# Seven-product tiles: two block sums by accumulating transfers, and 15 of 22 tiles instead of 12

## The chip, the cores and the metric
The kernel runs on one core of a Trainium2 chip. The metric is the device time of one execution in microseconds; lower is better. The engines are TensorE (PE), VectorE (DVE), ScalarE (ACT), GpSimd (POOL) and SyncE (SP), which issues most transfers; each works through its own instructions in order and waits for others by semaphores.

## What is computed
The reference is a two-layer model on 512 tokens of width 1024: in each layer a feed-forward part, a mixer (attention), and another feed-forward part, then a norm. The change touches the feed-forward parts alone:

```python
def _swiglu(x, w_gate, w_up, w_down):
    return (jax.nn.silu(x @ w_gate) * (x @ w_up)) @ w_down
...
    for l in range(DEPTH):
        x = x + 0.5 * _swiglu(_rms_norm(x, ffn1_norm[l]), ffn1_w_gate[l], ffn1_w_up[l], ffn1_w_down[l])
        h = _rms_norm(x, mix_norm[l])
        ...
        x = x + 0.5 * _swiglu(_rms_norm(x, ffn2_norm[l]), ffn2_w_gate[l], ffn2_w_up[l], ffn2_w_down[l])
```

All is float32. The inner width D_FF is 2816, which is 22 tiles of 128.

## The kernel before
The program runs the stages f0, e, f1, f2, m, f3: four feed-forward stages and two mixers. Activations lie transposed, features in the 128 partitions and 512 tokens in the columns. Each float32 factor is kept as a high part (rounded by a copy on ACT) and a low part (the rest, by a subtraction on DVE), and a product is three matmuls: high by high, low by high, high by low (`mm3`).

A feed-forward stage goes over 22 tiles f of the inner width, in two halves of 11. After each half the down projection of that half runs (264 matmuls). An ordinary tile loads its two weight tiles (gate and up, 512 KB each, names w, wh, wl), and makes 2 x 8 x 3 = 48 matmuls of 512 columns. For the tiles in the list `SEVEN`, gate and up together are taken as a matrix of 2 by 2 blocks A11, A12 (gate, first and second half of the width) and A21, A22 (up, R21 and R22 in the code), times the activations as 2 by 2 blocks, and are made by seven block products instead of eight, 7 x 4 x 3 = 84 matmuls of 256 columns. The products need A11, A12, A22 and four sums of weight blocks: S1 = R21 + R22, S2 = S1 + A11, S3 = A11 + R21, S4 = A12 + S2. Each of the seven then gets its high and its low part. The combined activations T12 and T34 are made once per stage (`combine`).

`chunk` hands out the weights in the order of use and fetches two entries of the list ahead of the one in use; a seven-product tile is one entry, an ordinary one two. The raw weights (w), their high parts (wh) and low parts (wl) have three buffers of 1024 columns each; a seven-product tile takes three pairs of wh and wl (A11 with S2, S1 with S3, A12 with S4) and a pair of its own for A22 (w3h, w3l, one buffer). The matmuls accumulate in PSUM banks pa, pb (two each), pt (three) and pc (one). A scheduler lays out each engine's instructions when the program is built, so the order on an engine is fixed, and an instruction that waits holds up all behind it on its engine.

Names that the steps below use: L160 and L161 split an ordinary weight tile (copy on ACT, low part on DVE); in `fetch_seven`, L170 and L171 load gate and up, L174 adds blocks on DVE, L180 and L181 split. In `seven`, L328 to L342 read the products out of PSUM (fm, fv, fn, fg) and L360, L376, L377 finish the tile. L251 is the power on GpSimd that makes a norm's factor, L231 its sums of squares. In the changed file lines from the end of `fetch_seven` on stand 13 lines further down, and the splits of a seven-product tile are L193 and L194.

Of the kernel before, what the change touches and what calls it, by code (L numbers as in the profile page):

```python
# [3 lines left out]
P = 128  # L4
D, SEQ, FF = 1024, 512, 2816
# [3 lines left out]
F32, F32R = mybir.dt.float32, mybir.dt.float32r  # L9
AF, OP, AX = mybir.ActivationFunctionType, mybir.AluOpType, mybir.AxisListType  # L10
# [14 lines left out]
def raw(ap):  # L25
    return ap.bitcast(F32)
# [2 lines left out]

SEVEN = (4, 5, 7, 8, 10, 11, 13, 14, 16, 17, 19, 20)

FFNS = {"f0": ("f1", 0, 0), "f1": ("f2", 0, 2), "f2": ("f1", 1, 3), "f3": ("f2", 1, 5)}

# [20 lines left out]
def flat(plan):  # L56
    return [u for _, fills in plan for f in fills for u in f.split()]


def keys(u):  # L60

    mla, c, n = u.isupper(), u[0].lower(), u[1:]
    if c == "v" and n in "aA":
        return [("ev_vsw", i) for i in range(3)]
    n = int(n)
    if mla:
        return {"L": [("mla_in", n)], "W": [("mla_uq", n)], "Y": [("mla_ukv", n)],
                "O": [("mla_out", n)]}.get(u[0], [])
    return {"q": [("ev_in", n)], "k": [("ev_in", n)], "s": [("ev_in", 4 + n)], "o": [("ev_out", n)],
            "c": [("cmp_w1", n, 0), ("cmp_w1", n, 1)], "v": [("ev_vb", n, 0), ("ev_vb", n, 1)]}.get(c, [])  # L70
# [7 lines left out]
class Core:  # L78
# [47 lines left out]
    def plan(self, stages):  # L126

        todo = []
        for st in stages:
            if st in FFNS:  # L130
                name, l, _ = FFNS[st]
                for h in range(2):
                    for f in range(h * HF, h * HF + HF):
                        if f in SEVEN:
                            todo.append(("seven", name, l, f))
                        else:
                            todo += [(name + "_g", l, f), (name + "_u", l, f)]
                    todo += [(name + "_d", l, h, c) for c in range(HF)]
            else:
                for u in flat(EVEN if st == "e" else MLA):  # L140
                    todo += keys(u)
        self.todo, self.ready, self.ahead = todo, [], 2

    def fetch(self):

# [15 lines left out]
        nc.vector.tensor_tensor(l[:, :cols], w[:, :cols], raw(h[:, :cols]), OP.subtract)  # L161
        self.ready.append((key, (h, l)))

    def fetch_seven(self, name, l, f):

        nc, kp, sb = self.nc, self.keep, self.sb
        g, u = [kp.tile([P, 1024], F32, name="w", bufs=3) for _ in range(2)]
        nc.sync.dma_start(g, self.a[name + "_g"][l, f])  # L170
        nc.sync.dma_start(u, self.a[name + "_u"][l, f])  # L171
        a11, a12, r21, r22 = g[:, :SEQ], g[:, SEQ:], u[:, :SEQ], u[:, SEQ:]
        s1, s2, s3, s4 = [sb.tile([P, SEQ], F32, name=f"s{i}") for i in range(1, 5)]
        add = lambda o, a, b: nc.vector.tensor_tensor(o, a, b, OP.add)  # L174
        out = {}

        def parts(blocks, h, l):
            for i, (n, src) in enumerate(blocks):
                c = slice(i * SEQ, i * SEQ + SEQ)
                nc.scalar.activation(h[:, c], src, AF.Copy)  # L180
                nc.vector.tensor_tensor(l[:, c], src, raw(h[:, c]), OP.subtract)  # L181
                out[n] = h[:, c], l[:, c]

        def pair():
            return [kp.tile([P, 1024], F32R, name=n, bufs=3) for n in ("wh", "wl")]
        add(s1, r21, r22)
        add(s2, s1, a11)
        parts((("A11", a11), ("S2", s2)), *pair())
        add(s3, a11, r21)
        parts((("S1", s1), ("S3", s3)), *pair())  # L190
        add(s4, a12, s2)
        parts((("A12", a12), ("S4", s4)), *pair())
        parts((("A22", r22),), *[sb.tile([P, SEQ], F32R, name=n) for n in ("w3h", "w3l")])  # L193
        return out  # L194

    def chunk(self, *key):
# [148 lines left out]
    def ffn(self, name, l, gi, then=None):  # L345

        nc = self.nc
        with self.tc.tile_pool(name="ff", bufs=1, reuse_waits="tile") as sb:
# [3 lines left out]
            for half in range(2):  # L352
                ah, al = [], []
                for i in range(HF):
                    f = half * HF + i
                    a = sb.tile([P, SEQ], F32, name="fa", bufs=2)
                    if f in SEVEN:
                        g, n = self.seven(sb, ("seven", name, l, f), xs, T, R)
# [607 lines left out]
def layout(np, i):  # L966

    i = {k: np.asarray(v) for k, v in i.items()}
    d = {"x": i["x"][0].T}
    d["g"] = np.concatenate(  # L970
        [v.reshape(-1, P).T for v in (i["ffn1_norm"][0], i["mix_norm"][0], i["ffn2_norm"][0], i["ffn1_norm"][1],
                                      i["mix_norm"][1], i["ffn2_norm"][1], i["final_norm"],
                                      i["mla_q_norm"][0], i["mla_kv_norm"][0])]
        + [np.zeros((P, 1), np.float32)], axis=1)
    for n in ("1", "2"):
        for s, t in (("gate", "g"), ("up", "u")):
            w = i[f"ffn{n}_w_{s}"]
            d[f"f{n}_{t}"] = w.reshape(2, KT, P, NF, P).transpose(0, 3, 2, 1, 4).reshape(2, NF, P, 1024)
        w = i[f"ffn{n}_w_down"].reshape(2, 2, HF, P, KT, P).transpose(0, 1, 4, 2, 3, 5)
        d[f"f{n}_d"] = w.reshape(2, 2, HF, 8, P, P).transpose(0, 1, 2, 4, 3, 5).reshape(2, 2, HF, P, 1024)  # L980

    def feat(w):

        k, n = w.shape[0] // P, w.shape[1] // P
        return w.reshape(k, P, n, P).transpose(2, 1, 0, 3).reshape(n, P, k * P)

    def out_parts(w, parts):

        w = w.reshape(8, P, KT, P)
        res = []  # L990
        for pairs in parts:
            n = len(pairs)
            v = w[list(pairs)].transpose(2, 0, 1, 3).reshape(n, 8, P, P)
            res.append(v.transpose(0, 2, 1, 3).reshape(n, P, 1024))
        return np.concatenate(res)

    def tok(w, n):

        w = w.reshape(KT, P, -1)
        pad = -KT % n  # L1000
        if pad:
            w = np.concatenate([w, np.zeros((pad,) + w.shape[1:], w.dtype)])
        return w.reshape(-1, n, P, w.shape[2]).transpose(0, 2, 1, 3).reshape(len(w) // n, P, -1)
    w = i["ev_w_in"][0]
    cols = [w[:, c:c + n] for c, n in ((C_QA, 512), (C_KC, 128), (C_VC, 128), (C_KS, 128), (C_KW, 128),
                                       (C_QB, 512), (C_KB, 512))]
    d["ev_in"] = feat(np.concatenate(cols, axis=1))
    d["ev_vsw"] = tok(np.concatenate([w[:, C_VS:C_VS + 128], w[:, C_VW:C_VW + 128], w[:, C_G:C_G + 24]], axis=1), 3)
    d["ev_vb"] = np.stack([tok(w[:, C_VB + 256 * j:C_VB + 256 * j + 256], 4) for j in range(2)])
    d["ev_out"] = out_parts(i["ev_w_out"][0], EV_PARTS)  # L1010
    w = np.stack([i[f"nsa_cmp_pos_{s}"][0].reshape(16, 2, 64).transpose(2, 1, 0) for s in "kv"], axis=1)
    d["pos"] = np.concatenate([w, w])
    d["cmp_w1"] = np.stack([i[f"nsa_cmp_{s}_w1"][0].reshape(2, 8, P, P).transpose(0, 2, 1, 3).reshape(2, P, 1024)
                            for s in "kv"])
    d["cmp_w2"] = np.stack([np.concatenate([i[f"nsa_cmp_{s}_w2"][0]] * 2, axis=1) for s in "kv"], axis=1)
    w = i["mla_w_in"][0]
    d["mla_in"] = feat(np.concatenate([w[:, :384]] + [w[:, 384:416]] * 4, axis=1))
    w = i["mla_w_uq"][0].reshape(2, P, 16, 96)
    n, r, z = w[..., :64], w[..., 64:], np.concatenate([w[..., 80:], w[..., 64:80]], axis=-1)
    w = np.stack([np.concatenate([n, r, z], axis=-1)[:, :, 0::2], np.concatenate([r, z, n], axis=-1)[:, :, 1::2]],  # L1020
                 axis=3)
    d["mla_uq"] = w.reshape(2, P, 4, 4, P).transpose(2, 1, 3, 0, 4).reshape(4, P, 1024)
    w = i["mla_w_ukv"][0].reshape(P, 2, 8, 2, 64).transpose(1, 0, 3, 2, 4)
    d["mla_ukv"] = w.reshape(2, P, 1024)
    d["mla_out"] = out_parts(i["mla_w_out"][0], ML_PARTS)
    d.update(constants(np))
    return {k: np.ascontiguousarray(v) for k, v in d.items()}
# [18 lines left out]
```

## Time and profile before
| | us |
|---|---|
| median of 3 runs | 1914.01 (1913.86 to 1915.62) |
| the profiled execution | 1913.86 |
| its span in the trace | 1911.7 |
| PE busy | 1883.0 |
| DVE busy | 1354.5 |
| ACT busy | 903.4 |
| POOL busy | 274.6 |

The span runs from the first to the last instruction of the trace; the execution's own time is 2.2 us longer. Busy shares are of the span. Starts in the timeline are counted from the span's start. An instruction's duration includes its pipeline, so neighbours overlap: what an instruction costs in a row of such is the distance between two starts.

### The profile page before, as it was taken

Reading aid. Unit: us, or ns where it says so; the run is one execution under the profiler, and the core shown is the slowest. Engines: PE = TensorE matmul, PEld = TensorE weight load, DVE = VectorE, ACT = ScalarE, POOL = GpSimd, SP = SyncE. Lnnn points to the kernel's source line nnn. Section 1 sums busy time; section 2 is a strip of 40 time slices with the busy share of each in tenths; the row PEclk is TensorE's granted clock in tenths of the full one; section 3 lists DMA queues with packets and bytes.
Section 4 is the critical chain, followed back from the end, with each engine's and each line's share of the span. In section 5 each row is a group of like instructions: output and inputs, shape, how many; then the busy total and the mean of one; then the engine's idle time right before and its main releaser. Section 6 shows DMA issues by size and latency. Waiting matters only on the chain. (4 is left out here: it accounts for less than half of the span.)

```text
span 1911.7 us, 27981 instructions
## 1 busy us (share of the span) xinstructions
PE 1883.0 (98%) x10850; PEld 1657.4 (87%) x10850; DVE 1354.5 (71%) x2438; ACT 903.4 (47%) x1585; POOL 274.6 (14%) x291
## 2 busy tenths in 40 slices
PE   9999999999999999999999999999999999999998
PEld 6998998878887789889988988998878879989987
DVE  8764875477888888468756864885489888747853
ACT  7432443347586654234435432443378664424432
POOL 0000000274454400000010000000156320000001
PEclk9999999999999999999999999999999999999999
DMA  4232333323111123323333232333311122333231
GB/s 170 86 113 87 110 98 109 118 89 93 58 45 34 45 85 114 100 89 109 111 92 96 82 118 89 100 108 102 123 39 33 56 89 89 111 99 100 89 110 67
DMA packets 49846, 174.67 MB, mean 91 GB/s; under 512 B 5793, under 2 KB 6049, under 8 KB 49713
## 3 DMA queue, kind: packets, MB, share of 16 engines
q1 hardware_dynamic: 48960, 171.74, 29.1%
q8 instruction: 85, 1.39, 0.3%
q10 hardware_dynamic: 720, 1.08, 0.2%
q14 instruction: 49, 0.39, 0.1%
q0 software_dynamic: 32, 0.07, 0.0%
HBM read 170.76 MB, written 2.10 MB: 90 GB/s over the span
## 5 line engine op out<-in xcount | busy, mean ns | idle before, releaser
L160 ACT ACTIVATE wh<-w 128x1024 fp32r<-128x1024 f32 (+1 forms) x217 | 229.2, 1057 | 357.7 <-PE pt L209 98.3
L161 DVE TENSOR_TENSOR wl<-w,wh 128x1024 fp32r<-128x1024 f32 (+1 forms) x217 | 273.0, 1259 | 159.4 <-ACT wh L160 158.3
L208 PE MATMUL pa<-xh,wh 128*128 128x512 f32 (+1 forms) x736 | 269.1, 366 | 2.8 <-ACT wh L160 2.2
L210 PE MATMUL pa<-xh,wl 128*128 128x512 f32 (+1 forms) x736 | 268.2, 364 | 0.5 <-DVE wl L161 0.5
L209 PE MATMUL pa<-xl,wh 128*128 128x512 f32 (+1 forms) x736 | 268.7, 365 | 0.0
L231 POOL TENSOR_TENSOR of<-of,t 128x512 f32<-128x512 f32 x36 | 55.9, 1552 | 1319.6 <-issue 892.5
L209 PE MATMUL pb<-xl,wh 128*128 128x256 f32 (+1 forms) x704 | 233.9, 332 | 0.2
L208 PE MATMUL pb<-xh,wh 128*128 128x256 f32 (+1 forms) x704 | 233.6, 332 | 0.0
L210 PE MATMUL pb<-xh,wl 128*128 128x256 f32 (+1 forms) x704 | 233.3, 331 | 0.0
L180 ACT ACTIVATE wh<-w 128x512 fp32r<-128x512 f32 x96 | 60.7, 632 | 237.9 <-PE pb L209 159.2
L208 PEld LDWEIGHTS pa<-xh,wh 128*128 128x128 f32 x736 | 139.9, 190 | 26.0 <-ACT wh L160 3.5
L210 PEld LDWEIGHTS pa<-xh,wl 128*128 128x128 f32 x736 | 139.7, 190 | 22.1 <-DVE wl L161 1.0
L209 PEld LDWEIGHTS pa<-xl,wh 128*128 128x128 f32 x736 | 139.9, 190 | 20.8 <-DVE xl L218 0.4
L209 PEld LDWEIGHTS pb<-xl,wh 128*128 128x128 f32 x704 | 133.8, 190 | 15.0 <-DVE xl L218 2.6
L208 PEld LDWEIGHTS pb<-xh,wh 128*128 128x128 f32 x704 | 133.8, 190 | 12.9 <-ACT xh L217 0.4
L210 PEld LDWEIGHTS pb<-xh,wl 128*128 128x128 f32 x704 | 133.8, 190 | 12.3
L180 ACT ACTIVATE wh<-s 128x512 fp32r<-128x512 f32 x192 | 114.9, 622 | 55.9 <-PE pa L209 26.3
L208 PE MATMUL pc<-fah,wh 128*128 128x512 f32 x352 | 137.0, 389 | 0.0
L209 PE MATMUL pc<-fal,wh 128*128 128x512 f32 x352 | 137.0, 389 | 0.0
L210 PE MATMUL pt<-fah,wl 128*128 128x512 f32 x352 | 136.9, 389 | 0.0
L210 PE MATMUL pc<-fah,wl 128*128 128x512 f32 x352 | 136.9, 389 | 0.0
L208 PE MATMUL pt<-fah,wh 128*128 128x512 f32 x352 | 136.9, 389 | 0.0
(264 smaller groups left out, 4556.3 us busy)
## 6 DMA issues: line engine op xcount, KB each, us to landing
w<-f_g SPq DMA_DIRECT2D x88, 512.0 KB, 3.7
w<-f_u SPq DMA_DIRECT2D x88, 512.0 KB, 3.6
w<-f_d SPq DMA_DIRECT2D x88, 512.0 KB, 3.7
w<-ev_in SPq DMA_DIRECT2D x16, 512.0 KB, 3.7
w<-ev_out SPq DMA_DIRECT2D x8, 512.0 KB, 3.3
w<-mla_out SPq DMA_DIRECT2D x8, 512.0 KB, 3.3
x<-x SPq DMA_DIRECT2D x8, 256.0 KB, 5.3
w<-ev_vb SPq DMA_DIRECT2D x4, 512.0 KB, 3.2
```

The costliest lines, as they stand in the source:

```text
L160: nc.scalar.activation(h[:, :cols], w[:, :cols], AF.Copy)
L161: nc.vector.tensor_tensor(l[:, :cols], w[:, :cols], raw(h[:, :cols]), OP.subtract)
L180: nc.scalar.activation(h[:, c], src, AF.Copy)
L208: nc.tensor.matmul(out, wh, xh, start=start, stop=False)
L209: nc.tensor.matmul(out, wh, xl, start=False, stop=False)
L210: nc.tensor.matmul(out, wl, xh, start=False, stop=stop)
L231: eng.tensor_tensor(parts[0], parts[0], sq, OP.add)
```

## The change
The host adds an array `f1_s` (and `f2_s`): for the tiles in `SEVEN`, 128 rows of A12, R22, A11, R21 side by side, 512 columns each. S1 and S3 are no longer added on DVE. `add_up` loads R21 twice into both halves of a tile s13 (two buffers; a plain transfer from SP), and then a transfer issued by GpSimd adds R22 | A11 to it on landing, so the tile holds S1 | S3. `fetch_seven` calls it for the next seven-product tile of the stage before it issues its own other loads; for the first one of a stage it calls it for both. A11, A12 and R22 come by three loads of 512 columns; S2 and S4 are still added on DVE, into the second halves of the tiles that hold A11 and A12. So the three pairs lie side by side and each is split by one instruction of 1024 columns on ACT and one on DVE. `SEVEN` lists 15 tiles instead of 12.

```diff
-SEVEN = (4, 5, 7, 8, 10, 11, 13, 14, 16, 17, 19, 20)
+SEVEN = (4, 5, 6, 7, 9, 10, 11, 12, 14, 15, 16, 17, 19, 20, 21)
...
-        self.todo, self.ready, self.ahead = todo, [], 2
+        self.todo, self.ready, self.ahead, self.sums = todo, [], 2, {}
...
+    def add_up(self, key):
+
+        name, l, f = key
+        u = self.sums[key] = self.sb.tile([P, 1024], F32, name="s13", bufs=2)
+        src = self.a[name + "_s"][l, SEVEN.index(f)]
+        self.nc.sync.dma_start(u.rearrange("p (a b) -> p a b", a=2),
+                               src[:, 3 * SEQ:].unsqueeze(1).to_broadcast([P, 2, SEQ]))
+        self.nc.gpsimd.dma_start(u, src[:, SEQ:3 * SEQ], accum_op=OP.add)
+
     def fetch_seven(self, name, l, f):
...
-        g, u = [kp.tile([P, 1024], F32, name="w", bufs=3) for _ in range(2)]
-        nc.sync.dma_start(g, self.a[name + "_g"][l, f])
-        nc.sync.dma_start(u, self.a[name + "_u"][l, f])
-        a11, a12, r21, r22 = g[:, :SEQ], g[:, SEQ:], u[:, :SEQ], u[:, SEQ:]
-        s1, s2, s3, s4 = [sb.tile([P, SEQ], F32, name=f"s{i}") for i in range(1, 5)]
-        add = lambda o, a, b: nc.vector.tensor_tensor(o, a, b, OP.add)
+        src = self.a[name + "_s"][l, SEVEN.index(f)]
+        u1, u3 = [kp.tile([P, 1024], F32, name="w", bufs=3) for _ in range(2)]
+        r22 = sb.tile([P, SEQ], F32, name="r22")
+        if not self.sums:
+            self.add_up((name, l, f))
+        u2 = self.sums.pop((name, l, f))
+        rest = [k[1:] for k in self.todo[len(self.ready) + 1:] if k[0] == "seven" and k[1:3] == (name, l)]
+        if rest:
+            self.add_up(rest[0])
+        nc.sync.dma_start(u1[:, :SEQ], src[:, 2 * SEQ:3 * SEQ])
+        nc.sync.dma_start(u3[:, :SEQ], src[:, :SEQ])
+        nc.sync.dma_start(r22, src[:, SEQ:2 * SEQ])
         out = {}
 
-        def parts(blocks, h, l):
-            for i, (n, src) in enumerate(blocks):
+        def parts(names, t, h, l):
+            nc.scalar.activation(h, t, AF.Copy)
+            nc.vector.tensor_tensor(l, t, raw(h), OP.subtract)
+            for i, n in enumerate(names):
                 c = slice(i * SEQ, i * SEQ + SEQ)
-                nc.scalar.activation(h[:, c], src, AF.Copy)
-                nc.vector.tensor_tensor(l[:, c], src, raw(h[:, c]), OP.subtract)
                 out[n] = h[:, c], l[:, c]
...
-        add(s1, r21, r22)
-        add(s2, s1, a11)
-        parts((("A11", a11), ("S2", s2)), *pair())
-        add(s3, a11, r21)
-        parts((("S1", s1), ("S3", s3)), *pair())
-        add(s4, a12, s2)
-        parts((("A12", a12), ("S4", s4)), *pair())
-        parts((("A22", r22),), *[sb.tile([P, SEQ], F32R, name=n) for n in ("w3h", "w3l")])
+        nc.vector.tensor_tensor(u1[:, SEQ:], u2[:, :SEQ], u1[:, :SEQ], OP.add)
+        parts(("A11", "S2"), u1, *pair())
+        parts(("S1", "S3"), u2, *pair())
+        nc.vector.tensor_tensor(u3[:, SEQ:], u3[:, :SEQ], u1[:, SEQ:], OP.add)
+        parts(("A12", "S4"), u3, *pair())
+        parts(("A22",), r22, *[sb.tile([P, SEQ], F32R, name=n) for n in ("w3h", "w3l")])
...
+        g, u = d[f"f{n}_g"][:, list(SEVEN)], d[f"f{n}_u"][:, list(SEVEN)]
+        d[f"f{n}_s"] = np.concatenate([g[..., SEQ:], u[..., SEQ:], g[..., :SEQ], u[..., :SEQ]], axis=-1)
```

How the change orders the engines' work is shown at three places of stage f0. The first is DVE around the start of tile 4, the first one by seven products. Before (s1 to s4 with 523 to 526 and w_519, w_520 belong to tile 5; w_460 and s4_467 to tile 4; fa and fal to the ordinary tile 3):

```order
L174 TENSOR_TENSOR s1_523<-w_520 128x512
L174 TENSOR_TENSOR s3_525<-w_519,w_520 128x512
L174 TENSOR_TENSOR s2_524<-s1_523,w_519 128x512
L373 TENSOR_TENSOR fa_459<-pb_553,fg_578 128x512
L181 TENSOR_TENSOR wl_485<-w_460,wh_484 128x512
L181 TENSOR_TENSOR wl_485<-s4_467,wh_484 128x512
L377 TENSOR_TENSOR fal_583<-fa_459,fah_582 128x512
L174 TENSOR_TENSOR s4_526<-w_519,s2_524 128x512
L181 TENSOR_TENSOR wl_530<-w_519,wh_529 128x512
```

and now (s13_463 and w_461 belong to tile 4, w_515 and s13_466 to tile 5, w_576 and s13_518 to tile 6):

```order
L194 TENSOR_TENSOR wl_478<-s13_463,wh_477 128x1024
L386 TENSOR_TENSOR fa_459<-pb_542,fg_567 128x512
L194 TENSOR_TENSOR wl_483<-w_461,wh_482 128x1024
L390 TENSOR_TENSOR fal_572<-fa_459,fah_571 128x512
L201 TENSOR_TENSOR w_576<-s13_518,w_576 128x512
L194 TENSOR_TENSOR wl_526<-w_515,wh_525 128x1024
L343 TENSOR_TENSOR fv_608<-fm_609,pa_603 128x256
L194 TENSOR_TENSOR wl_530<-s13_466,wh_529 128x1024
L346 TENSOR_TENSOR fm_609<-fv_608,pt_605 128x512
```

The three additions of tile 5 are gone from here, and the addition of tile 6, which needs the accumulating transfer into s13_518, now stands ahead of the low parts of tile 5.

The second place is the queue of SP over the same tiles. Before (tiles 4 and 5, then an ordinary one):

```order
L170 DMA w_460<-f1_g 128x1024
L171 DMA w_461<-f1_u 128x1024
L170 DMA w_519<-f1_g 128x1024
L171 DMA w_520<-f1_u 128x1024
L154 DMA w_587<-f1_g 128x1024
```

and now (u1 and u3 of tiles 4, 5 and 6 are w_460 and w_461, w_515 and w_516, w_576 and w_577):

```order
L187 DMA w_460<-f1_s 128x512
L188 DMA w_461<-f1_s 128x512
L187 DMA w_515<-f1_s 128x512
L188 DMA w_516<-f1_s 128x512
L169 DMA s13_518<-f1_s 128x2x512
L187 DMA w_576<-f1_s 128x512
L188 DMA w_577<-f1_s 128x512
L169 DMA s13_579<-f1_s 128x2x512
```

Two loads a tile have become four, and the base of tile 6 (s13_518) is issued ahead of u1 of that tile, as soon as s13_463 is free.

The third place is PE where a tile that comes right behind another seven-product tile goes from A11's product to S1's. Before, in tile 5:

```order
L209 MATMUL pa_705<-xl_125,wh_529 128x256
L210 MATMUL pa_705<-xh_124,wl_530 128x256
L208 MATMUL pt_707<-T12h_257,wh_536 128x256
L209 MATMUL pt_707<-T12l_259,wh_536 128x256
L210 MATMUL pt_707<-T12h_257,wl_537 128x256
L208 MATMUL pt_707<-T12h_257,wh_536 128x256
```

and now in tile 6 (wh_586 is A11 with S2, wh_590 and wl_591 are S1 with S3, wh_595 is A12 with S4):

```order
L222 MATMUL pa_848<-xl_125,wh_586 128x256
L223 MATMUL pa_848<-xh_124,wl_587 128x256
L221 MATMUL pt_850<-T12h_257,wh_590 128x256
L222 MATMUL pt_850<-T12l_259,wh_590 128x256
L221 MATMUL pb_849<-xh_128,wh_595 128x256
L222 MATMUL pb_849<-xl_129,wh_595 128x256
L223 MATMUL pt_850<-T12h_257,wl_591 128x256
```

The third matmul of S1's product, the first one that reads the low part of S1, has moved behind two matmuls of A12's product.

## Rows read from the trace of the kernel before

**Rows 1.** The page, part 1: busy us of each engine, share of the span, instructions.
```profile
PE 1883.0 (98%) x10850; PEld 1657.4 (87%) x10850; DVE 1354.5 (71%) x2438; ACT 903.4 (47%) x1585; POOL 274.6 (14%) x291
```

**Rows 2.** Waits of PE, then of DVE: us in total, times, longest.
```profile
PE pb L609 <- DVE mn L412: 3.8, 4, 2.3
PE pb L209 <- DVE kl L837: 2.4, 1, 2.4
...
DVE s L174 <- DMA w<-f_u: 17.1, 5, 3.8
```

**Rows 3.** Timeline of PE: start, duration in us; the first matmuls of tiles.
```profile
56.28 0.28 PE L208 MATMUL pa<-xh,wh 128*128 128x256 f32 x1
...
66.35 0.28 PE L208 MATMUL pa<-xh,wh 128*128 128x256 f32 x1
...
76.43 0.40 PE L208 MATMUL pa<-xh,wh 128*128 128x512 f32 x1
...
87.34 0.28 PE L208 MATMUL pa<-xh,wh 128*128 128x256 f32 x1
...
1786.57 0.28 PE L208 MATMUL pa<-xh,wh 128*128 128x256 f32 x1
...
1796.65 0.40 PE L208 MATMUL pa<-xh,wh 128*128 128x512 f32 x1
...
1807.56 0.28 PE L208 MATMUL pa<-xh,wh 128*128 128x256 f32 x1
```

**Rows 4.** Groups by form: busy us, mean ns; then timeline of DVE.
```profile
L161 DVE TENSOR_TENSOR wl<-w,wh 128x1024 fp32r<-128x1024 f32 x214 | 267.8, 1252 | 158.1 <-ACT wh L160 157.1
...
L160 ACT ACTIVATE wh<-w 128x1024 fp32r<-128x1024 f32 x214 | 226.5, 1059 | 353.6 <-PE pt L209 98.3 <-PE pc L209 91.8 <-issue 71.5
...
105.28 1.22 DVE L161 TENSOR_TENSOR wl<-w,wh 128x1024 fp32r<-128x1024 f32 x1
106.41 0.41 DVE L335 TENSOR_TENSOR fn<-fm,pt 128x256 f32<-128x256 f32 x1
106.74 0.68 DVE L338 TENSOR_TENSOR fg<-fm,pb 128x512 f32<-128x512 f32 x1
107.34 0.68 DVE L181 TENSOR_TENSOR wl<-w,wh 128x512 fp32r<-128x512 f32 x1
```

**Rows 5.** Timeline of ACT in the tile that starts at 87.34; wait and releaser in brackets.
```profile
91.78 0.63 ACT L180 ACTIVATE wh<-w 128x512 fp32r<-128x512 f32 x1 [2.42 <-PE pt L209]
...
93.17 1.15 ACT L180 ACTIVATE wh<-s 128x512 fp32r<-128x512 f32 x2 [0.24 <-PE pa L209]
96.05 0.63 ACT L180 ACTIVATE wh<-w 128x512 fp32r<-128x512 f32 x1 [1.73 <-PE pb L209]
```

**Rows 6.** Transfers: count, KB each, median us to landing; then one issue on POOL.
```profile
w<-f_g SPq DMA_DIRECT2D x88, 512.0 KB, 3.7
...
x<-x SPq DMA_DIRECT2D x8, 256.0 KB, 5.3
...
CQ<-cs_q SPq DMA_DIRECT2D x2, 256.0 KB, 4.1
...
ident<-ident POOLq DMA_DIRECT2D x1, 64.0 KB, 3.8
...
1.23 0.76 POOL L108 DMA_DIRECT2D ident<-ident  x1 [0.79 <-POOLq L1038]
```

**Rows 7.** Windows: length, busy (count) of PE, PEld, DVE, ACT, POOL; clock, DMA share, GB/s.
```profile
66.40:76.40 10.00, 10.00 (x85) 10.00 (x85) 7.87 (x14) 4.92 (x7) 0.00 (x0) 1.00 0.53 159
```

**Rows 8.** Timeline of PE at a gap in stage e; then the window behind it.
```profile
417.08 0.50 PE L609 MATMUL pb<-kh,q 128*128 128x512 f32 x1 [2.30 <-DVE mn L412]
...
418.20:421.60 3.40, 3.40 (x11) 2.73 (x10) 2.47 (x6) 1.88 (x6) 3.28 (x3) 0.50 0.20 43
```

**Rows 9.** Window over most of stage m; timeline of POOL at the start of f1.
```profile
1404.50:1540.00 135.50, 134.46 (x770) 117.38 (x768) 116.50 (x311) 102.45 (x241) 67.57 (x84) 1.00 0.15 48
...
671.59 1.14 POOL L251 TENSOR_TENSOR rcol<-rv,mhalf 128x4 f32<-128x4 f32 x1 [5.41 <-DVE rv L246]
```

## The prediction

> **What bounds the kernel now.** I read the busy shares first: TensorE (PE) is busy for 1883.0 of 1911.7 us [rows 1]. Then PE's own waits: the two largest belong to attention lines (L609, L209 with kl), and the longest single wait is 2.4 us [rows 2]. In the gate/up loops of the four feed-forward stages PE doesn't wait at all once the kernel's first 16 us are over: the window of one tile there shows it busy for 10.00 of 10.00 us at a granted clock of 1.00, which is the upper level of 2.4 GHz [rows 7]. So the time there is what PE needs per tile, and the timeline of PE gives that by the tiles' first matmuls [rows 3]. A tile by seven products starts at 56.28, the next at 66.35 and ends at 76.43: 10.08 us (84 matmuls of 256 columns, 0.12 us apart). The ordinary tile from 76.43 to 87.34 takes 10.91 us (48 matmuls of 512 columns, 0.227 us apart). Near the end of the kernel the lengths are the same (1786.57 to 1796.65 to 1807.56). A seven-product tile is therefore worth 0.83 us, as long as its weights are ready.
>
> **What the change takes away.** SEVEN grows from 12 to 15 tiles a stage, in four stages: 12 more tiles, 12 x 0.83 = 10.0 us of PE time, all of it on the path.
>
> **VectorE (DVE).** Its pitch from one instruction to the next is 1.13 us for 1024 columns, 0.33 for 256, 0.60 for 512 [rows 4]. A seven-product tile before: 4 sums and 7 low halves of 512 columns, 11 x 0.60 = 6.6, and reading the products (3 instructions of 256 columns, 5 of 512) 3 x 0.33 + 5 x 0.60 = 4.0; together 10.6, more than PE's 10.08, so DVE fell behind in each pair and caught up in the ordinary tile. After: 2 sums and A22's low half at 512 columns (1.8), three low halves of 1024 (3.4), the same 4.0: 9.2 us. DVE no longer forbids four such tiles in a row. ScalarE copies three wide pieces of 1.06 us instead of six narrow ones and has less to do than DVE. These edits cost nothing; PE's 10.08 us cover them.
>
> **Transfers by size.** Before, a tile took two loads of 512 KB. Now it takes three of 256 KB, a base of 512 KB (one block of 256 KB written twice) and the accumulating transfer of 512 KB: 1.84 million bytes. A window with such loads moved 159 GB/s at a share of 0.53 [rows 7], which is 300 GB/s at full share: 6.1 of the tile's 10.08 us, and 7.9 if the accumulation also fetches its destination. It fits, with less room than before. The queue of SyncE issues 4 loads a tile instead of 2, no bound either.
>
> **The new wait.** S1|S3 is now made by a chain: SyncE loads the base when one of two buffers of s13 is free; GpSimd waits for that landing and issues the accumulation; DVE's addition that makes S2 (L201) waits for that. DVE runs in order, and behind that addition stand the low half of the previous tile's A11|S2, its L343 on a product, and the low half of the previous tile's S1|S3, which frees the buffer for the next base. In a run of such tiles the chain closes on itself. Let A be the time from the base's landing to the accumulation's landing, and 0 the start of the first tile (tile 4, say) of a run of four.
> - Tile 4's S1|S3 takes the weight buffer of tile 3's gate half, free at -5.45 (half of 10.91); copy 1.06, low half 1.25 [rows 4]: its s13 buffer is free at -3.1. The base of tile 6 lands 3.7 later [rows 6], at 0.6, its accumulation at A + 0.6.
> - DVE runs the addition (0.60), the low half of tile 5's A11|S2 (1.13), L343 (0.33) and the low half of tile 5's S1|S3 (1.13): done at A + 3.8, but not before 8.1, since the weight buffers of a running tile come free 4.44, 5.83 and 8.71 us after its start at 87.34 [rows 3, 5] and this pair takes the second (5.83 + 1.06 + 1.25).
> - The base of tile 7 lands at A + 7.5, its accumulation at 2A + 7.5. Then L201 0.60, L390 0.60, L343 0.33 and tile 6's S1|S3 1.25: 2A + 10.3.
> - PE wants that low half in tile 6, which starts at 20.16, after A11's product (12 matmuls, 1.44) and four more matmuls (0.48): at 22.1.
>
> So PE waits where A is over 5.9 us, and then for 2(A - 5.9) in each run of four. There are two such runs a stage (4 to 7, 14 to 17), eight in all. Tiles 8 and 18 are ordinary and give the chain over 10 us back, so nothing is carried on. The run 19 to 21 has the first turn alone: A + 0.6 + 0.60 + 1.13 must be under 10.08, A under 7.7. The pairs around the down projection have more room.
>
> **How large is A?** No accumulating transfer is in the trace. From below: a plain load of as many bytes, 3.7 us; nothing in an accumulation can make it shorter. From above: one such load for the destination's fetch and one for the block, 7.4. Between them: the only transfer that GpSimd issues, 64 KB, lands 3.8 us after its issue (0.76 of that on GpSimd), beside a burst in which loads of x took 5.3 where 256 KB otherwise take 4.1 [rows 6]. With 448 KB more at 300 GB/s (1.5) that makes 5.3. I take it, as the row of the same queue is the nearest; the destination's fetch (up to 1.7) and the burst (about 1.2 too much) pull in opposite directions. 2 x 5.3 + 10.3 = 20.9 leaves 1.2 us before PE waits. DVE itself will wait for the accumulation; it waits for loads now, five times, the longest 3.8 us [rows 2], and PE felt none of it.
> By the Trainium skill (DMA: Bandwidth & Descriptors, "Anatomy of one DMA — SWDGE (gpsimd) path") a transfer issued by GpSimd takes about 2.0 us plus its bytes at 436 GB/s, an estimated 3.2 us for 512 KB, under which no run waits and the sum stays. The trace's 64 KB took 3.8 where that rule makes 2.2, so I keep to the row.
>
> **Moved instructions.** In the first three feed-forward stages GpSimd's queue holds two accumulations ahead of the L264 that makes the norm's factor. GpSimd is idle for 5.41 us before that instruction [rows 9]; two issues of 0.76 are hidden there if their bases have landed, and those are loaded early. The mixer "e" keeps PE's order; in "m" PE's rows come in another order from the middle on. PE idles there for 135.5 - 134.46 = 1.0 us [rows 9], so -1 at best, and I allow +3.
>
> **Rivals.** (1) **Slower**: the accumulation is slow, A of 6.8 or more. Place: the low half of S1|S3 in the third tile of each run of four. At A = 7.4 a run loses 3.0 us, 8 x 3.0 = 24, time 1913.9 - 10.0 + 24 = 1928. If such gaps also cost clock, as after the 2.30 us gap that has 3.4 us at half clock behind it (0.50, the level of 1.2 GHz [rows 8], 1.7 us lost), 8 x 1.7 more: 1941. It decides where 16(A - 5.9) passes 10.0 + 3.8, at A = 6.8. For it: two landings in series where there was one. Against: the row that gives 5.3. Chance 0.26.
> The same page of the Trainium skill, "Rules for kernel authors", says that an accumulating transfer reads its destination and writes it later, so that the earlier transfer's semaphore must be awaited; no run here shows one yet. It is the series that this rival counts.
> (2) A between 6.3 and 6.8: the runs lose 6 to 14 us and eat the gain, 1910 to 1918. With it goes the case that the queue at the stages' starts holds L264 back by some us each. Chance 0.12.
> (3) The change doesn't do what it says because the transfers together set the pace and not PE. 7.9 of 10.08 us speaks against it; it would show as a longer A and is counted in (1).
>
> **How the numbers follow.** The sum goes against the profiled execution of 1913.86 us (span 1911.7 and 2.2 around it; the median of the runs is 1914.01): 1913.86 - 9.96 = 1903.9, say 1904. Chance of this case (A up to 6.3, PE waits of at most 6 us in all) 0.62, from 1902 (1 us out of "m", one more for what I round) to 1910. To hold the time 8 times in 10 the range must reach into the slow case up to A = 7.4: 1902 to 1928. A measurement of this kernel can tell about 0.2% (3.8 us) from no change: faster 0.62, same 0.12, slower 0.26.
>
> **What would show it.** Right: tiles of 10.08 us in runs of four, no waits of PE in the loops, L201 on DVE waiting some us at most for the accumulation, A of 4 to 6 us. Wrong: PE waiting for the low half (L194) or the copy (L193) of s13, gaps of 2 us and more in tiles 6 and 16, a drop of the granted clock behind them, or DMA shares over 0.8 in the runs.

## The result, and the profile after

The changed kernel takes 1982.02 us (median, 1980.64 to 1986.12) where the kernel before, beside it on the same chip, takes 1914.42: a ratio of 1.0356 (1.034 to 1.0373). It is slower by 68 us; I had forecast 1904 with a range of 1902 to 1928, so neither the sign nor the range held.

The page of the changed kernel: part 1 (busy us, share, instructions; to be read against [rows 1]), then parts 3 and 6 (queues: packets, MB, share of the 16 engines; transfers: count, KB each, median us from issue to landing):
```profile
PE 1903.5 (96%) x11282; PEld 1691.0 (85%) x11282; DVE 1350.5 (68%) x2306; ACT 912.2 (46%) x1477; POOL 324.0 (16%) x351
...
q1 hardware_dynamic: 73920, 187.47, 30.5%
q0 software_dynamic: 8672, 31.53, 9.6%
...
s<-f_s SPq DMA_DIRECT2D x60, 512.0 KB, 4.3
s<-f_s POOLq DMA_DIRECT2D x60, 512.0 KB, 6.9
```
The span is 1984.4 us. PE was to be busy for 10 us less than before; it is busy for 20.5 us more, and its share still falls, from 98% to 96%. The accumulating transfer takes 6.9 us from issue to landing.

The waits of PE in the changed kernel, then of DVE (us in total, times, longest), against [rows 2]:
```profile
PE pt L223 <- DVE wl L194: 27.0, 8, 3.7
PE pa L223 <- DVE wl L194: 14.3, 12, 2.7
PE pb L223 <- DVE wl L194: 8.2, 9, 1.0
...
DVE w L201 <- DMA s<-f_s: 109.9, 20, 7.5
```
All three largest waits of PE are for a low part of a seven-product tile (L194), 49.5 us together; none of them was there before. DVE in turn waits for the accumulating transfer at L201, where it makes S2.

Where the 72.7 us between the two spans lie is told by windows over the stages: f0, then f1 with f2, then m, then f3 (length, busy us and count of PE, PEld, DVE, ACT, POOL, granted clock, DMA share, GB/s). The kernel before:
```profile
16.20:409.80 393.60, 393.60 (x2278) 349.18 (x2278) 264.47 (x400) 162.16 (x243) 34.64 (x28) 1.00 0.34 103
654.10:1395.50 741.40, 741.15 (x4263) 655.18 (x4263) 504.37 (x771) 309.64 (x467) 35.30 (x27) 1.00 0.33 100
1395.50:1542.30 146.80, 141.48 (x793) 123.15 (x793) 126.30 (x329) 108.33 (x254) 71.34 (x88) 0.98 0.14 44
1542.30:1911.70 369.40, 361.36 (x2098) 319.87 (x2098) 248.08 (x383) 147.69 (x224) 21.37 (x14) 0.99 0.31 95
```
The changed kernel:
```profile
16.70:429.30 412.60, 399.66 (x2386) 359.52 (x2386) 262.45 (x367) 164.18 (x216) 46.84 (x42) 0.98 0.45 124
674.00:1449.10 775.10, 749.90 (x4479) 671.92 (x4479) 501.78 (x705) 314.19 (x413) 61.15 (x57) 0.98 0.47 126
1449.10:1601.50 152.40, 144.43 (x795) 123.38 (x794) 127.79 (x330) 108.97 (x256) 69.93 (x90) 0.98 0.19 55
1601.50:1984.40 382.90, 362.94 (x2206) 325.07 (x2206) 246.50 (x349) 148.92 (x196) 32.76 (x27) 0.99 0.43 117
```
The feed-forward stages are longer by 19.0, 33.7 and 13.5 us where they were to be shorter by 2.5, 5.0 and 2.5. In f0 PE was busy without a break before (393.60 of 393.60); now it idles for 12.9 us, and its granted clock is 0.98. Stage m, which has no seven-product tile, is longer by 5.6 us too. The matmuls of 256 columns alone don't make this: the experiments below bring f0 to 391.2.

The run of four tiles 4 to 7 in f0: the first matmul of each tile on PE, and the largest gap, in the changed kernel (start, duration; in brackets the wait and what ended it), against [rows 3]:
```profile
56.82 0.28 PE L221 MATMUL pa<-xh,wh 128*128 128x256 f32 x1
...
66.89 0.28 PE L221 MATMUL pa<-xh,wh 128*128 128x256 f32 x1
...
79.11 0.28 PE L221 MATMUL pa<-xh,wh 128*128 128x256 f32 x1
...
84.76 0.58 PE L223 MATMUL pt<-T12h,wl 128*128 128x256 f32 x1 [3.56 <-DVE wl L194]
...
95.31 0.28 PE L221 MATMUL pa<-xh,wh 128*128 128x256 f32 x1
```
Tile 4 takes the 10.07 us it should. Tile 5 takes 12.22, tile 6 takes 16.20: 6.1 us too long, of which 3.56 are the gap. The rest is clock, as the windows of tile 6 and of the stretch behind its gap show (columns as above):
```profile
79.10:95.30 16.20, 12.63 (x86) 12.43 (x85) 11.22 (x18) 5.18 (x7) 0.86 (x1) 0.79 0.60 155
...
85.30:88.70 3.40, 3.40 (x18) 3.40 (x17) 3.40 (x7) 0.28 (x1) 0.00 (x0) 0.50 0.62 176
```
PE was idle for 3.56 us; behind that the granted clock is 0.50, the level of 1.2 GHz, and the same 86 matmuls take 12.63 busy us instead of 10.1. The other runs of four in the kernel look alike: the first line of the waits above counts eight of these gaps, one in the third tile of each run, 2.69 to 3.70 us long. Behind seven of them the granted clock is 0.50; behind the one in f3's first run (3.07 us, up to 1678.82) it is 1.00.

What DVE does meanwhile (timeline of DVE, then of SP's DMA queue and of POOL, changed kernel):
```profile
66.03 0.69 DVE L201 TENSOR_TENSOR w<-s,w 128x512 f32<-128x512 f32 x1 [6.26 <-DMA s<-f_s]
66.64 1.22 DVE L194 TENSOR_TENSOR wl<-w,wh 128x1024 fp32r<-128x1024 f32 x1
...
68.10 1.22 DVE L194 TENSOR_TENSOR wl<-s,wh 128x1024 fp32r<-128x1024 f32 x1
...
81.94 0.69 DVE L201 TENSOR_TENSOR w<-s,w 128x512 f32<-128x512 f32 x1 [4.20 <-DMA s<-f_s]
...
83.49 1.22 DVE L194 TENSOR_TENSOR wl<-s,wh 128x1024 fp32r<-128x1024 f32 x1
```
```profile
55.37 0.38 SPq L169 DMA_DIRECT2D s<-f_s  x1
...
69.35 0.38 SPq L169 DMA_DIRECT2D s<-f_s  x1
...
60.12 0.93 POOL L171 DMA_DIRECT2D s<-f_s  x1 [31.88 <-DVE fal L390]
74.51 0.87 POOL L171 DMA_DIRECT2D s<-f_s  x1 [13.46 <-DVE w3l L194]
```
Follow one turn. The low part of tile 5's S1|S3 (68.10, done at 69.3) frees a buffer of s13; the base for tile 7 is issued at 69.35; GpSimd issues the accumulation at 74.51 (POOL waited for the base, not for what the bracket names, which was done long before); L201 of tile 7 starts at 81.94; behind it on DVE stands tile 6's S1|S3 at 83.49, which frees the next buffer. From one S1|S3 to the next that is 15.4 us, where PE uses up a tile in 10.08. What the low part of tile 6's S1|S3 itself needs was there long before: its high part, ACT's copy, was done at 77.96, and DVE did nothing from 77.75 to 81.94 but wait at L201.

### The profile page after: what moved, and what is told of

Read it like the earlier page. It is cut to its first block, busy times and chain, and to the rows that moved or that the text cites. A ratio compares the mean times of both kernels' runs of the same rounds, so it can differ in the third digit from the quotient of the medians.

```text
span 1984.4 us, 29122 instructions
## 1 busy us (share of the span) xinstructions
PE 1903.5 (96%) x11282; PEld 1691.0 (85%) x11282; DVE 1350.5 (68%) x2306; ACT 912.2 (46%) x1477; POOL 324.0 (16%) x351
## 3 DMA queue, kind: packets, MB, share of 16 engines
q0 software_dynamic: 8672, 31.53, 9.6%
## 5 line engine op out<-in xcount | busy, mean ns | idle before, releaser
L160 ACT ACTIVATE wh<-w 128x1024 fp32r<-128x1024 f32 x193 | 204.0, 1058 | 304.8 <-PE pc L222 94.1
L161 DVE TENSOR_TENSOR wl<-w,wh 128x1024 fp32r<-128x1024 f32 x193 | 244.6, 1268 | 105.1 <-ACT wh L160 104.5
L223 PE MATMUL pa<-xh,wl 128*128 128x512 f32 (+1 forms) x688 | 246.0, 358 | 14.8 <-DVE wl L194 14.3
L221 PE MATMUL pa<-xh,wh 128*128 128x512 f32 (+1 forms) x688 | 245.8, 357 | 4.3 <-ACT wh L160 2.3
L222 PE MATMUL pa<-xl,wh 128*128 128x512 f32 (+1 forms) x688 | 244.9, 356 | 0.0
L221 PE MATMUL pb<-xh,wh 128*128 128x256 f32 (+1 forms) x704 | 224.4, 319 | 0.5 <-ACT wh L160 0.5
L222 PE MATMUL pb<-xl,wh 128*128 128x256 f32 (+1 forms) x704 | 224.2, 318 | 0.2
L171 POOL DMA_DIRECT2D s<-f_s x60 | 52.4, 877 | 1044.5 <-DVE fg L405 261.7
L193 ACT ACTIVATE wh<-w 128x1024 fp32r<-128x1024 f32 x120 | 126.7, 1056 | 142.3 <-PE pb L222 62.6
L194 DVE TENSOR_TENSOR wl<-w,wh 128x1024 fp32r<-128x1024 f32 x120 | 146.6, 1222 | 31.0 <-ACT wh L193 31.0
L221 PEld LDWEIGHTS pa<-xh,wh 128*128 128x128 f32 x688 | 130.8, 190 | 24.4 <-ACT wh L160 3.5
L201 DVE TENSOR_TENSOR w<-s,w 128x512 f32<-128x512 f32 x60 | 41.5, 691 | 142.0 <-DMA s<-f_s 109.9
```

Of the source, the lines that this page charges most:

```text
L160: nc.scalar.activation(h[:, :cols], w[:, :cols], AF.Copy)
L171: self.nc.gpsimd.dma_start(u, src[:, SEQ:3 * SEQ], accum_op=OP.add)
L193: nc.scalar.activation(h, t, AF.Copy)
L194: nc.vector.tensor_tensor(l, t, raw(h), OP.subtract)
L201: nc.vector.tensor_tensor(u1[:, SEQ:], u2[:, :SEQ], u1[:, :SEQ], OP.add)
L221: nc.tensor.matmul(out, wh, xh, start=start, stop=False)
```

## The experiments

Three theories. (1) The chain: S1|S3 of tile n stands on DVE behind the addition (L201) of tile n+1, which waits for a base, an accumulation and a free buffer in series. (2) Load: the transfers as such slow the loads, DVE or PE. (3) Four such tiles in a row are more than DVE can do, whatever the loads.

**No accumulation.** The transfer is left out:
```
-        self.nc.gpsimd.dma_start(u, src[:, SEQ:3 * SEQ], accum_op=OP.add)
```


> The GpSimd transfer is left out, so s13 holds R21 twice and S1, S3, S2, S4 are not the sums; all else stands as in the changed kernel. Theory 1 (the 70 us are a serial chain: base landing 4.3 us, then the accumulation 6.9 us from its issue, and DVE's L201 waits for it with other low parts behind it): the chain loses its longer link, PE waits in the gate/up loops fall from about 50 us to under 3, time 1903 to 1908. Theory 2 (the 16 transfer engines are short of time): also faster, since the accumulation took 9.6 of the 40 per cent that the two queues hold, but the remaining loads still land late, 1910 to 1940. Theory 3 (runs of four seven-product tiles are too much for DVE or for the queue of SP whatever is summed): 1960 or more.

1911.52 us (1910.56 to 1914.51; ratio 0.9982, 0.9973 to 0.9991). PE has no gap in the feed-forward loops, as the window over f0 shows:
```profile
16.45:407.65 391.20, 391.19 (x2386) 352.40 (x2386) 263.35 (x367) 164.34 (x216) 34.61 (x28) 1.00 0.36 110
```
The fifteen tiles in runs of four are not the cause (against theory 3), the accumulation is; but by load or by chain this run doesn't tell. The time is over the 1903 to 1908 that I had given for the chain; where the rest lies is told under the order of m below.

**The same transfer without the addition.**
```
-        self.nc.gpsimd.dma_start(u, src[:, SEQ:3 * SEQ], accum_op=OP.add)
+        self.nc.gpsimd.dma_start(u, src[:, SEQ:3 * SEQ])
```


> The GpSimd transfer is plain: it overwrites s13 with R22 and A11 instead of adding, so the sums are wrong, but every wait stands. Theory 1: a packet of 4 KB falls from 328 ns to 159 as in plain loads, 8 per engine make 1.35 us, so issue to landing goes from 6.9 to about 5.5 us, and a run of four loses 2 x 1.35 us less plus its drop of the clock: 1920 to 1945. Theory 2: fewer microseconds of engine time by 95 us in all, spread over 60 tiles; 1960 to 1980.

One run, 1922.67 us. The queues and the transfer on its page, then the waits of PE:
```profile
q1 hardware_dynamic: 73920, 187.47, 31.1%
q0 software_dynamic: 8672, 31.53, 5.0%
...
s<-f_s POOLq DMA_DIRECT2D x60, 512.0 KB, 4.9
```
```profile
PE pt L223 <- DVE wl L194: 6.3, 7, 1.3
...
PE pb L223 <- DVE wl L194: 3.1, 3, 1.7
```
The transfer lands after 4.9 us instead of 6.9. Seven gaps stand where they stood, in the third tiles of the runs, three more in second tiles; together they are 9.4 us instead of 49.5, none is over 1.73 us, and the granted clock doesn't fall behind any of them. Adding is what makes the transfer longer: the same 31.53 MB of GpSimd's queue (q0) hold the engines for 5.0% of the span here and for 9.6% in the changed kernel.

**The accumulation beside the chain**, into a tile that nobody reads:
```
-        self.nc.gpsimd.dma_start(u, src[:, SEQ:3 * SEQ], accum_op=OP.add)
+        self.nc.gpsimd.dma_start(self.aside, src[:, SEQ:3 * SEQ], accum_op=OP.add)
```
(The tile is made and set to zero once a stage; fah and fal get 11 buffers instead of 12 to make room.)

> The accumulating transfer goes into a tile of its own that nobody reads, so its load on the transfer engines stays whole and only the wait of L201 for it is gone; s13 holds R21 twice, the sums are wrong. (The buffers of fah and fal go from 12 to 11 to make room.) Theory 1: 1904 to 1910, PE waits in the loops under 5 us. Theory 2: 1965 or more, loads land as late as in the changed kernel and PE waits for them.

1935.67 us (ratio 1.0106, 1.0086 to 1.0126), in neither of the two ranges given. This one isn't clean. The waits of PE, and a row of POOL:
```profile
PE pt L273 <- POOL rcol L264: 8.2, 1, 8.2
PE pt L223 <- DVE wl L194: 4.4, 5, 1.7
```
```profile
1583.59 1.38 POOL L264 TENSOR_TENSOR rcol<-rv,mhalf 128x4 f32<-128x4 f32 x1
```
Since all accumulations go to one tile, each waits for the one before, on GpSimd (8.82 us for the one issued at 1583.02), and behind them stands L264, which makes a norm's factor: PE waited 8.2 us for it. That is the second rival's mishap; in the changed kernel it didn't happen. The loops have small gaps only (waits for L194, 8.4 us in all). The run speaks for the chain but can't price the load.

**Everything as in the changed kernel, but DVE's order.** L201 is put behind the previous tile's low part of S1|S3 instead of ahead of it (excerpt; `low13` is that low part):
```
+        prev = self.low13
+        with self.tc.issue_after(prev) if prev is not None else nullcontext():
             nc.vector.tensor_tensor(u1[:, SEQ:], u2[:, :SEQ], u1[:, :SEQ], OP.add)
...
-        parts(("S1", "S3"), u2, *pair())
+        self.low13 = parts(("S1", "S3"), u2, *pair()).ins
```


> Everything is computed, with all transfers; only L201, the addition that waits for the accumulation, is put on DVE behind the low part of S1 and S3 of the tile before. Theory 1: what is late is not the transfer itself but what stands behind L201 on DVE and what that frees; from the s13 buffer's release (8.1 us into a tile) 4.3 + 0.5 + 6.9 us make 19.8, while the sum is needed about 30 us after the same start; PE waits nearly vanish, 1904 to 1915. Theory 2: no change of the transfers, 1970 to 1985. Theory 3: 1970 to 1985 too.

1911.63 us (1910.37 to 1915.32; ratio 0.998, 0.997 to 0.999): the 70 us are gone, with every transfer in place. Timeline of DVE in the same run of four, then the windows over f0, f1 with f2, m and f3:
```profile
64.71 1.22 DVE L197 TENSOR_TENSOR wl<-s,wh 128x1024 fp32r<-128x1024 f32 x1
65.84 0.68 DVE L207 TENSOR_TENSOR w<-s,w 128x512 f32<-128x512 f32 x1
...
76.35 1.22 DVE L197 TENSOR_TENSOR wl<-s,wh 128x1024 fp32r<-128x1024 f32 x1
...
78.12 0.69 DVE L207 TENSOR_TENSOR w<-s,w 128x512 f32<-128x512 f32 x1 [0.55 <-DMA s<-f_s]
```
```profile
17.60:408.80 391.20, 391.18 (x2386) 352.38 (x2386) 262.95 (x367) 163.50 (x216) 46.56 (x42) 1.00 0.47 130
654.20:1390.70 736.50, 736.26 (x4479) 661.58 (x4479) 501.94 (x705) 313.38 (x413) 60.69 (x57) 1.00 0.48 133
1390.70:1543.00 152.30, 143.78 (x793) 122.60 (x793) 127.71 (x330) 108.74 (x256) 69.75 (x90) 0.99 0.19 56
1543.00:1910.60 367.60, 359.17 (x2206) 323.06 (x2206) 247.03 (x349) 148.98 (x196) 32.48 (x27) 0.99 0.44 122
```
The accumulation still takes 6.7 us and the base 4.1. But the low part of S1|S3 (L197 here) now goes first, and the addition of the next tile (L207) behind it waits for half a microsecond. A turn of the chain (base, accumulation, addition, S1|S3) spans two tiles of PE, 20.16 us, and fits. f0 is 391.20 us, as without the accumulation (391.20 there as well), and f1 with f2 takes 736.50 us in both, so the load costs nothing that shows. Theory 2 falls; the cause is the place of L201 on DVE. The scheduler moved some of DVE's other instructions, of ACT's copies and of PE's products along with it. PE's order is not what helps: the low part of tile 6's S1|S3 is done at 77.57, before tile 6 starts on PE at 77.85.

**Pairs instead of runs of four**, in the changed kernel:
```
-SEVEN = (4, 5, 6, 7, 9, 10, 11, 12, 14, 15, 16, 17, 19, 20, 21)
+SEVEN = (4, 5, 7, 8, 10, 11, 13, 14, 16, 17, 19, 20)
```


> The changed kernel with the twelve tiles a stage of the kernel before, which come in pairs: accumulating transfers, but never a third such tile in a row. Left out: nothing. Chain of waits (theory 1): the two buffers of s13 both come free in the ordinary tile between two pairs, so the loop does not close on itself; at most gaps of 1 to 2 us in some pairs' second tiles, as the second tile of a run of four had; 1911 to 1922 us. Load of the transfers (theory 2): each tile by seven products pays the same, 12/15 of the loss of some 70 us, so 1960 to 1970.

1915.23 us, ratio 1.0001 (0.9992 to 1.0011). The window over f0:
```profile
17.50:411.50 394.00, 393.92 (x2278) 349.06 (x2278) 247.45 (x340) 158.86 (x207) 44.22 (x39) 1.00 0.44 123
```
The 48 accumulations land after 6.5 us, L201 has the place that it has in the changed kernel, and PE doesn't wait in the loops: the ordinary tile between two pairs gives the chain its time back. So the loss needs both, the chain and the run.

**A third buffer**, with the sums issued two tiles ahead and L201 where the changed kernel has it:
```
-        u = self.sums[key] = self.sb.tile([P, 1024], F32, name="s13", bufs=2)
+        u = self.sums[key] = self.sb.tile([P, 1024], F32, name="s13", bufs=3)
...
-        if rest:
-            self.add_up(rest[0])
+        for k in rest[:2]:
+            if k not in self.sums:
+                self.add_up(k)
```


> The changed kernel with three buffers of s13 instead of two and the sums issued two tiles ahead (fah and fal have 11 buffers instead of 12, to make room). DVE's addition L201 keeps its place ahead of the previous tile's S1|S3. Left out: nothing. Chain of waits: with a third buffer the base no longer waits for the S1|S3 of the tile just ahead, so the accumulation has some 10 us more and L201 finds it done; no waits of PE of 2 us or more in the loops, 1908 to 1914 (stage m has the longer order). If the transfers' load, or the mere place of L201, makes the loss: 1960 and more, with the gaps in the third tiles still there.

1919.31 us, ratio 1.0021 (1.0012 to 1.003). The gaps of the third tiles are gone, though an accumulation now takes 7.3 us; that part came as the chain expects. The time is 5 us above what I had given. PE has a new wait where m goes over into f3, 4.3 us long (the waits of PE, then the timeline of ACT there):
```profile
PE pa L222 <- DVE x L550: 5.9, 5, 4.3
```
```profile
1547.20 0.63 ACT L194 ACTIVATE w3h<-r 128x512 fp32r<-128x512 f32 x1 [7.57 <-DMA r<-f_s]
```
ACT stands at the copy of an A22 until its load lands, and DVE at the low part behind it. That load was issued at 1536.42, right behind three bases that went out together (1534.98), and three accumulations followed at 1541.5 to 1547.1. More buffers moved the hold-up to another place. That wait is not all of it: f0 and f1 with f2 take 394.30 and 740.10 us, 3.1 and 3.6 more than in d1_order, and why is not taken apart.

**Fifteen tiles in the kernel before**, with plain loads and four sums on DVE:
```
-SEVEN = (4, 5, 7, 8, 10, 11, 13, 14, 16, 17, 19, 20)
+SEVEN = (4, 5, 6, 7, 9, 10, 11, 12, 14, 15, 16, 17, 19, 20, 21)
```


> The kernel before with the fifteen tiles of the changed one: all four sums on DVE from plain loads, no accumulating transfer. Left out: nothing. Chain of waits: without the transfers there is no chain; DVE needs 10.6 us a tile against 10.08 of PE, so a run of four costs it some 2 us, which the ordinary tile behind gives back. 1914 less 10.0, plus 5.5 for the other order of PE's rows in stage m (which this kernel shares), plus 0 to 8 for DVE: 1909 to 1918. If runs of four as such, with DVE, were what costs time (theory 3): 1960 and more.

1909.82 us (ratio 0.9971, 0.9959 to 0.9983). No wait in the loops; f0 takes 391.20 us:
```profile
16.30:407.50 391.20, 391.18 (x2386) 352.37 (x2386) 282.18 (x442) 169.05 (x261) 34.41 (x28) 1.00 0.34 103
```
DVE's 10.6 us a tile against PE's 10.08 were no reason to take sums off it, in runs of four.

**The order of m.** Without the accumulation, with DVE's order mended and with the old sums, stage m takes 152.1, 152.3 and 151.2 us against 146.80 before; the one run with fifteen tiles where PE's rows of m stand as before is a3_aside. The scheduler lays m out by what stands ahead of it. A sixteenth tile in the stage ahead of m alone brings the old order nearly back. To d1_order, and to b2_old15, this is added:
```
-SEVEN = (4, 5, 6, 7, 9, 10, 11, 12, 14, 15, 16, 17, 19, 20, 21)
+SEVEN = (4, 5, 6, 7, 8, 9, 10, 11, 12, 14, 15, 16, 17, 19, 20, 21)
+PLAIN = (('f1', 0, 8), ('f2', 0, 8), ('f2', 1, 8))
...
-                        if f in SEVEN:
+                        if f in SEVEN and (name, l, f) not in PLAIN:
```


> d1_order with a sixteenth tile by seven products (tile 8) in the stage ahead of m alone, which brings PE's rows of m back close to the order of the kernel before. Left out: nothing. If the order of m is worth the 5.5 us by which that stage is longer: 1911.6 less 5.5 less 0.8 for the tile, 1904 to 1907, and the stretch between m's first and last wait of PE at 146 to 148 us. If the stage is longer for the transfers or the clock: 1910 to 1912, the stretch at 151 to 152.

> b2_old15 (all sums on DVE from plain loads, fifteen tiles) with a sixteenth tile in the stage ahead of m alone, which brings PE's rows of m close to the order of before, as in d2_m_order. Left out: nothing. If the order of m costs 5.5 us whatever the loads are: 1909.8 less 5.5 less 0.8, 1902 to 1906, and the stretch between m's first and last wait of PE at 146 to 147 us. It also tells what the accumulating transfers are worth when nothing waits for them: against d2_m_order (1906.4) no more than 2 us either way. If m's length hangs on the transfers: 1908 to 1911.

The first gives 1906.38 us (1905.8 to 1907.35; ratio 0.9955, 0.9939 to 0.9972), the second 1904.69 (1904.0 to 1907.13; ratio 0.9949, 0.9937 to 0.9962). The window over m in each, and in b2_old15:
```profile
1390.10:1536.90 146.80, 141.40 (x795) 122.97 (x794) 127.92 (x330) 108.59 (x256) 73.20 (x90) 0.98 0.19 56
```
```profile
1389.40:1535.70 146.30, 140.93 (x794) 122.62 (x794) 127.23 (x329) 107.97 (x255) 71.57 (x88) 0.99 0.14 44
```
```profile
1389.90:1541.10 151.20, 143.60 (x794) 122.83 (x794) 127.35 (x329) 108.23 (x255) 67.88 (x88) 0.99 0.14 43
```
The order of PE's rows in m is worth about 5 us, with transfers or without; a4_pairs, which has the transfers and the order of before, takes 147.10 us there. And the runs of the two kernels overlap: sums by transfer gain nothing over sums on DVE that these runs can tell. b5_old_m, the kernel before with longer runs, has the lowest median of all, and all that the change does to loads and sums can be left out.

**Longer runs with the mended order**: d1_order with
```
+SEVEN = (4, 5, 6, 7, 8, 9, 10, 11, 12, 13, 14, 15, 16, 17, 19, 20, 21)
```


> d1_order with seventeen tiles by seven products in each stage (4 to 17 and 19 to 21), whose rows in m come in the order of the kernel before. Left out: nothing. If only DVE's order made the changed kernel slow, a run of fourteen works as a run of four: 1911.6 less 5.5 for m less 8 tiles of 0.83, 1898 to 1902, no waits of PE in the loops. If long runs have a loss of their own (the transfers, or a lag of DVE that grows): 1910 and more, with gaps late in the run.

1922.21 us (1912.90 to 1923.05), ratio 1.0026 (1.0008 to 1.0045): not the 1898 to 1902 of the first case but the second case, a loss of long runs themselves. The waits of PE, then of DVE:
```profile
PE pb L229 <- DVE wl L197: 11.3, 15, 1.2
...
DVE w L207 <- DMA s<-f_s: 45.7, 28, 3.5
```
PE waits again, from the fifth or sixth tile of a run on (the down projection after tile 10 parts the fourteen tiles into two runs of seven), and DVE's addition waits for the accumulation again, in 28 places. GpSimd issues them 9.3 to 12.4 us apart in f0's first run (57.36 to 111.73: 10.9 on average), more than PE's 10.08. So the mended order puts the limit off; it doesn't lift it. Which link is the longest there is not shown.

## Why the prediction was wrong, point by point

**What held.** PE sets the time, and a seven-product tile is worth 0.83 us: f0, f1 with f2, and f3 shrink by 2.4, 4.9 and 2.5 us in b2_old15 (366.90 us for f3), 9.8 of the forecast 9.96. DVE's and ACT's own work hides; it did so with the old sums too (b2_old15), so DVE was no bound on runs of four before. The bytes fit: DMA share 0.47 in f0, with no loss in d1_order. L264 isn't held up in the changed kernel. The chain was drawn as it is, with its eight runs, its place (the low part of S1|S3 in the third tile) and the half clock behind all but one of the eight gaps. What I called rival (1) is what happened.

**The step that failed: the size of A**, from the base's landing to the accumulation's. I took 5.3, from a row of 64 KB on the same queue plus 1.5 for the further bytes, and had 7.4 as the upper bound. Measured are 6.9 from GpSimd's issue alone, and the issue comes some 0.55 us behind the base's landing, which makes 7.4; in the two turns above it is 6.4 (59.55 to 65.95) and 8.0 (73.95 to 81.92), from the landing of a base that takes 4.2 and 4.6 us. The nearest row was the wrong kind: it priced the queue, not the addition. Two transfers of the size in question, the bound that I put aside, was right, and a2_plain_gpsimd shows why: an accumulated byte holds the engines nearly twice as long. I had that in the sum of bytes (7.9 of 10.08 us); beside A I named it, up to 1.7 us, but set it off against a burst around the 64 KB transfer. The form of the sum held: with these landings put in, it has the low parts of S1|S3 done at 69.1 for tile 5 and 84.7 for tile 6, and 69.3 and 84.7 are measured. And A of this size costs time only with this order on DVE: in d1_order the accumulation takes 6.7 us and nothing waits for it long.

On the rule put beside A: the Trainium skill (DMA: Bandwidth & Descriptors, "Anatomy of one DMA — SWDGE (gpsimd) path") makes an estimated 3.2 us for 512 KB; measured are 4.9 plain and 6.9 accumulating, and the measurement decides.

**The start of the chain.** I had the buffer free 3.1 us ahead of tile 4 and a base landing in 3.7. The base was issued 1.45 ahead (55.37 against 56.82), since DVE stood 2.22 us at the addition of S4 for another of the new loads, and it landed in 4.2; GpSimd issued half a microsecond later. So L201 of tile 6 started 9.2 us into the run, against 5.9 in my sum.

**The price of the rival.** The eight third-tile gaps cost 27.0 us; I had 24 at A = 7.4. What I missed is the other 22.5 us (pa and pb in the waits): the second tiles of the runs and the run 19 to 21, which were to be safe with A under 7.7. They weren't, with the chain starting some 2 us later. And 13.6 us of clock were allowed for, outside the range; against d1_order PE is busy for 8.5, 13.6 and 3.8 us more in the three stretches, 25.9 in all, for the same matmuls. Together: 49.5 of waits and 25.9 of clock make 75.4, and the spans of the changed kernel and of d1_order differ by 73.8.

**Stage m.** I allowed -1 to +3 us for its new order; it costs about 5. The order was known before the run. I had bounded it by PE's idle time in the old order, which says what a better order may gain and nothing of what a worse one may lose.

**The chances.** The rival had 0.26 for A of 6.8 or more. The bounds of A were 3.7 and 7.4, no row of the trace between them was of an accumulation, and by my own sum the change turned from gain to loss at 6.8, inside these bounds. The range should have carried the upper end through with its clock, 1941, and even that would have been too low.

## What to carry to other kernels

When an instruction on an in-order engine comes to wait for a chain of transfers, look at what the scheduler has put behind it: if that frees the buffer from which the chain starts, the chain closes on itself and its length, not the engine's work, is the pitch of the loop. Price it with every landing in series, and take the upper bound of a transfer that the trace doesn't show if the sign hangs on it. Try the cheap half of a change alone first: here longer runs without new transfers gave all there was to gain.

## What the runs showed of the hardware

- An accumulating transfer of 512 KB from GpSimd lands 6.9 us after its issue (6.5 to 7.3 in the other kernels, 5.9 into the tile that nobody reads), a plain one of the same blocks in the same queue 4.9; the base, issued by SyncE with the same 512 KB, takes 4.3 (all medians). The accumulating bytes hold the DMA engines for 9.6% of the span instead of 5.0% (of spans of 1984.4 and 1920.9 us: 2.0 times the time).
- A gap of 3.56 us on PE was followed by a granted clock of 0.50 (the level of 1.2 GHz) in the window behind it, and tile 6 lost 2.5 us to it. Seven of the eight third-tile gaps were followed by that level; the one of 3.07 us in f3's first run was followed by 1.00. Behind the gaps of a2_plain_gpsimd, up to 1.73 us, the clock in the loops stayed at 1.00. So the changed kernel lost clock (25.9 us against d1_order) on top of its waits, and a2_plain_gpsimd its 9.4 us of waits without it.
